# Moving the routing's rank steps, pairing the gathers, and giving the last scatter four banks, in a two-layer decoder trunk with expert routing

## The chip, the cores and the metric

The kernel runs on one core of a Trainium2 chip. The time is the device time of one execution in microseconds (us). The engines are PE (TensorE: matmuls and transposes), DVE (VectorE), ACT (ScalarE), POOL (GpSimd) and SP (SyncE, whose queue issues all weight transfers). PE loads its stationary operand in an instruction of its own (PEld). Results of PE land in PSUM, which has eight banks of 128 x 512 fp32 numbers; DVE and ACT read them from there.

## The reference, cut to what matters

One sequence of 256 tokens with 1024 channels goes through an RWKV-7 time mix, a dense SwiGLU, an RG-LRU block and an expert layer, and a last norm. The change is in the expert layer:

```python
def moe_swiglu(h, w_router, b_router, w_gu, w_d):
    t = h.reshape(B * T, D)
    logits = (t @ w_router + b_router).astype(jnp.float32)
    top_v, top_i = lax.top_k(logits, TOP_K)                      # 2 of 8
    probs = jax.nn.softmax(top_v, axis=-1)
    comb = jnp.einsum('nk,nke->ne', probs, jax.nn.one_hot(top_i, N_EXPERTS))
    out = jnp.zeros_like(t)
    for e in range(N_EXPERTS):
        out = out + comb[:, e, None] * swiglu(t, w_gu[e], w_d[e])  # (silu(g) * u) @ w_d
```

Its output, times a gate, is added to the residual x, and x is normed. All numbers are fp32.

## The kernel before, in words

**Experts and steps.** The router ranks the eight logits of each token; the two best are the token's experts. An expert gets a table of up to 128 tokens. The first expert is fixed (FIRST, expert 7 of the reference). The other seven are ranked by their token counts, and `TURN` gives the order of turns: turns 0, 2, 4, 6 are "big" (tables of 128 tokens), turns 1, 3, 5, 7 (`SMALL`) are "small" (64 tokens). Each turn's hidden width of 3584 is cut into seven pieces of 512, so there are 56 steps (e, j); `steps` lists three big ones and then a small and a big one in turn. A small and a big step are called a pair below. Step (e, j) needs 6 MB of weights, in the order in which `st.add` lists them: the gate and up half, then the down half of the step before.

**One step.** A big step multiplies with weights that are split in two: ACT casts a piece (`wh`), DVE subtracts it from the original (`wl`), and three products with the split tokens (`xh`, `xl`) give 24 matmuls into bank `mg` and 24 into `mu` (`gu_half`, line 2037). A small step multiplies with the raw weights `rw`, 64 columns at a time, gate and up side by side in one bank `mg` (`gu_small`, line 2047): eight groups k of two products, which the trace records as four. Then follow SiLU, the product with the up half (`sl`), four transposes into `hp` (`tpose`, line 2070), their copy to SBUF as `hTh` (ACT) and `hTl` (DVE) in `tparts`, and the second projection `dn` (`down`, line 2138). Step s does its own first projection and, at its end, `down(s - 1)`.

**The order.** Work beside the projections is hung into a plan: `put(s, n, f)` (line 2091) runs f in step s behind its group n (`tick`). Groups 0 to 7 are those of the first projection, 8 to 11 those of `down`. Each engine runs its instructions in the order in which the program issues them, and a weight cast is issued when the stream (`Stream`, line 104) reaches the piece, up to four pieces ahead. `InOrder` forbids the scheduler to reorder while its flag is on, which it is from the routing seam on.

**The routing seam.** The first expert's gather (`first_gather`, line 1816) fills two banks `gp`; ACT and DVE copy them out in turns as `rr` and split them. On DVE the counts `cnt` are copied first, then `softmax` (line 1776) prepares the weights of the two chosen experts. `t_rank` (line 1967, five small instructions on a 7 x 7 table) ranks the experts and `t_sel` (line 1976, ten) turns the ranks into the order of turns, `turn_i`, which SP loads into registers to address the weights from step 3 on. `t_rank` is put at (0, 1) and `t_sel` at (0, 3), inside the first expert step.

**Gathers.** In steps (1, 4), (3, 4) and (5, 4) the next two experts' tokens are gathered. `gather(e, k, w)` (line 2016) is eight products with a one-hot matrix `Pm` into one PSUM bank; `gathered` (line 2028) copies it out on ACT and DVE: two halves for the big expert (`cst` or `other`), two for the small one (`condr`), and the split. There are four such groups, k = 0, 2, 4, 6, at groups 0, 1, 2, 3 of the step, their copies one group later. Their tiles, those of `hp`, of `ptp` (`scatter_cols`, line 1943) and of the scatters carry the tag "m", which alternates between two banks (line 1938). In small steps `tpose` and `tparts` stand at group 4.

**The last scatter.** The last expert's output is multiplied back to token order in four products, two column halves by two token halves (`scatter`, line 2119), and added to x in `onto`. At the end of the program `onto_last` (line 2267) runs product and addition together, one after the other.

Of the kernel before, what the change touches and what calls it, by code (L numbers as in the profile page):

```python
# [7 lines left out]
F32 = mybir.dt.float32  # L8
# [3 lines left out]
AF = mybir.ActivationFunctionType  # L12
ALU = mybir.AluOpType
AX = mybir.AxisListType
PSUM = bass.MemoryType.PSUM

P = 128
# [7 lines left out]
E = 8  # L25
CAP = 128
# [4 lines left out]
HALF = 64  # L31

LEAD = 3

TURN = (3, 0, 4, 1, 5, 2, 6)
# [321 lines left out]
def kernel_body(tc, io, out, dbg=None):  # L357
# [18 lines left out]
    with ctx:  # L376
# [1202 lines left out]
        for c2 in range(4):  # L1579
            ps = lin("x", c2)  # L1580
# [195 lines left out]
        def softmax():  # L1776

            V.tensor_scalar(o1, rank, 0.0, None, ALU.is_equal)
            V.tensor_scalar(o2, rank, 1.0, None, ALU.is_equal)
            V.tensor_reduce(m1, lg, AX.X, ALU.max)  # L1780
            V.tensor_tensor(cmb, o2, lg, ALU.mult)
            V.tensor_reduce(m2, cmb, AX.X, ALU.add)
            V.tensor_tensor(m2, m1, m2, ALU.subtract)
# [53 lines left out]
        def root(i):  # L1837
            S.activation(rs[i], rs[i], AF.Sqrt, bias=eps_n, scale=1.0 / D)

        st.held = []  # L1840
        lo_mm(1, 1, 0, last[0])
        res(0)
# [43 lines left out]
        first_gather(1, range(4), range(1, 2))  # L1886
        first_gather(1, range(4, 8))
        V.tensor_copy(cnt, pps[1][:, E:2 * E])
        softmax()
        lx.close()  # L1890
        dump("x3", xt)
        dump("lg", lg)
# [33 lines left out]
        for k2 in range(5):  # L1926
# [5 lines left out]
            if k2 == 3:  # L1932
                more(1)
                later()

        S.activation(m2, m2, AF.Tanh, scale=0.5)
        st.held = None
        pdn = Turn(pa.pool, bank, m=[4, 5], dn0=[7], dn1=[0], dns=[6])
        pgu = Turn(pa.pool, bank, g=[1], u=[3], gs=[2])
# [17 lines left out]
            onehot(Pms[e], i, e)  # L1957

        Pm2 = {}


        N7 = E - 1
        o7 = oscr.rearrange("p a b c -> p (a b c)")[:, 0:N7 * N7].rearrange("p (b c) -> p b c", b=N7)

        RK = V

        def t_rank():

            a_, b_ = cnt[:, None, 0:N7].broadcast_to([P, N7, N7]), cnt[:, 0:N7, None].broadcast_to([P, N7, N7])
            RK.tensor_tensor(o7, a_, b_, ALU.is_equal)  # L1970
            RK.tensor_tensor(o7, o7, lt8[:, 0:N7, 0:N7], ALU.mult)
            RK.tensor_tensor(sel, a_, b_, ALU.is_gt)
            RK.tensor_tensor(o7, o7, sel, ALU.add)
            RK.tensor_reduce(crank, o7, AX.X, ALU.add)

        def t_sel():
            for k, r in enumerate(TURN):
                RK.tensor_scalar(sel[:, k, :], crank, float(r), None, ALU.is_equal)
            RK.tensor_tensor(o7, sel, iota[:, None, 0:N7].broadcast_to([P, N7, N7]), ALU.mult)
            RK.tensor_reduce(turnf, o7, AX.X, ALU.add)  # L1980
            RK.tensor_copy(turn_i, turnf)

        def t_sort(dst, src):
            V.tensor_copy(dst[:, :, 0:1], src[:, :, FIRST:E])
# [31 lines left out]
        def gather(e, k0, w):  # L2016

            gp[e, k0] = ps = pdn.tile([P, 2, w], F32, tag="m", name=f"gp{e}{k0}", bufs=2)
            for kk in range(2):
                for z, src in enumerate((hh, hl)):  # L2020
                    for i in range(2):
                        mm(ps[:, kk, :], src[:, i, (k0 + kk) * P:(k0 + kk + 1) * P], Pm2[e][:, i, 0:w], z == 0 and i == 0, z == 1 and i == 1)
# [68 lines left out]
        def put(s, n, *fs):  # L2091
            plan.setdefault((s, n), []).extend(fs)
# [5 lines left out]
        def expert_out(e):  # L2098


            yg, parts, ps = {}, {}, {}
            small = e in SMALL
            rows_ = [slice(n * HALF, (n + 1) * HALF) if small else slice(0, P) for n in range(2)]

            def weigh(n):
                yg[n] = other if small or n == 0 else spare
                r = rows_[n]
                V.tensor_tensor(yg[n][r], dps[e][0 if small else n][r], gt2[r, n * 512:(n + 1) * 512], ALU.mult)

            def split(n):  # L2110
                yh = mb.tile([P, 512], F32R, tag="yh", name=f"yh{e}{n}", bufs=1)
                yl = mb.tile([P, 512], F32R, tag="yl", name=f"yl{e}{n}", bufs=1)
                S.copy(yh, yg[n])
                V.tensor_tensor(yl, yg[n], yh.bitcast(F32), ALU.subtract)
                parts[n] = yh, yl
                if small:
                    parts[1] = parts[n]

            def scatter(n, i):
                r = rows_[n]  # L2120
                ps[n, i] = pdn.tile([P, 512], F32, tag="m", name=f"sc{e}{n}{i}", bufs=2)
                l = PTs[e][r, i, :]
                if e == E - 1:
                    mm(ps[n, i], l.bitcast(F32), yg[n][r], True, True)
                else:
                    mm(ps[n, i], l, parts[n][0][r], True, False)
                    mm(ps[n, i], l, parts[n][1][r], False, True)

            def onto(n, i):
                sl = slice(n * 512, (n + 1) * 512)  # L2130
                V.scalar_tensor_tensor(xt[:, i, sl], ps[n, i], cmbq[:, i, e:e + 1], xt[:, i, sl], ALU.mult, ALU.add)

            return [[lambda n=n, f=f: f(n) for n in range(2)] for f in (weigh, split)] + [
                {(n, i): (lambda n=n, i=i, f=f: f(n, i)) for n in range(2) for i in range(2)} for f in (scatter, onto)]
# [36 lines left out]
                S.copy(gt2[:, n * 512:(n + 1) * 512], gt2ps[n])  # L2171

        at = {x: k for k, x in enumerate(steps)}
        put(0, 1, t_rank)
        put(0, 3, t_sel)
        put(0, 6, lambda: t_sort(posq, posm))
        put(1, 0, lambda: t_sort(mskq, msk))

# [13 lines left out]
        for e in SMALL:  # L2192

            if e > 1:
                w, p, sc, add = outs[e - 2]
                t = at[e, 0]
                put(t, 0, *w)
                put(t, 1, p[0])
                for i in range(2):
                    put(t, 6 + 3 * i, *(f[n, i] for f in (sc, add) for n in range(2)))  # L2200
            put(at[e, 1], 2, lambda e=e: scatter_cols(e, V.tensor_copy))
            if e > 1:
                put(at[e, 3], 2, lambda e=e: scatter_cols(e - 1, V.tensor_copy))

            w, p, sc, add = outs[e - 1]
            t = at[e, 8 - LEAD]
            put(t, 0, w[0])
            put(t, 1, p[0], w[1])
            put(t, 6, p[1])
            for n, k in zip((3, 5, 8, 10), sc):  # L2210
                put(t, n, sc[k], add[k])

            if e < E - 1:
                for i in range(2):
                    put(at[e, 3], 5 + i, lambda e=e, i=i: choice(e + 1, i))
                    put(at[e, 3], 8 + i, lambda e=e, i=i: choice(e + 2, i))
                for k in range(0, KT, 2):
                    put(at[e, 7 - LEAD], k // 2, lambda e=e, k=k: gather(e + 1, k, CAP + HALF))
                    put(at[e, 7 - LEAD], k // 2 + 1, lambda e=e, k=k: gathered(e + 1, k))
        w7, _, sc7, add7 = outs[E - 1]  # L2220

        gus = {}
        for s, (e, j) in enumerate(steps):
            now[0] = s
            small = e in SMALL
            gus[s] = [pgu.tile([P, 512], F32, tag="gs" if small else "g", name=f"mg{s}")]
            if s > 0:
                put(s, 4 if small else 1, lambda s=s: tpose(s - 1))
                put(s, 4 if small else 2, lambda s=s: tparts(s - 1))
            if small:  # L2230
                gu_small(e, gus[s][0])
                silu(s)
                times(s)
            else:
                put(s, 5, lambda s=s: silu(s))
                if s > 0:
                    put(s, 9, lambda s=s: times(s))
                gu_half(e, gus[s][0], 0)
            if s == 0:
                scatter_cols(0, S.copy)  # L2240
                weights()
                rx.close()
                mp = ctx.enter_context(tc.tile_pool(name="moe", bufs=1, side="right"))
                mb = ml.enter_context(tc.tile_pool(name="moe3", bufs=1, side="right"))
                gt2 = mp.tile([P, D], F32, name="mgt2")
                st.behind = None
            if not small:
                gus[s].append(pgu.tile([P, 512], F32, tag="u", name=f"mu{s}"))
                gu_half(e, gus[s][1], 4)
            if s == 0:  # L2250
                st.load()
                turns()
            if s == len(steps) - 1:
                down(s - 1, range(2))
                tpose(s)
                tparts(s)
                down(s - 1, range(2, 4))
                down(s)
                preload(AF.Sqrt)
                for f in w7:  # L2260
                    f()
            elif s > 0:
                down(s - 1)
            else:
                times(0)
        assert not plan, plan.keys()
        onto_last = {k: lambda k=k: (sc7[k](), add7[k]()) for k in sc7}

        o = rawC.tile([P, 2 * D], F32, tag="raw", name="fo").rearrange("p (i d) -> p i d", i=2)

# [155 lines left out]
```

## Time and profile before

| | us |
|---|---|
| time, median of 3 runs (1482.25 to 1483.77) | 1483.29 |
| the profiled execution: its own time | 1483.4 |
| its span, first to last instruction | 1481.6 |
| PE busy | 1418.6 (96%) |
| DVE busy | 1015.3 (69%) |
| ACT busy | 755.4 (51%) |
| weights moved | 488.53 MB |

The experts take from about 619 us to 1467 us. Nearly all instructions are recorded by one helper, so their line is L99 and they are told apart by their tiles. Matmuls are pipelined, and a PE that is "busy" is not at its peak, so the start times in the chain of waits say more than the busy sums. Of two engines with little idle time the chain tells which one the other waits for.

### The profile page before, as it was taken

What the parts mean: (1) busy time and instruction counts of PE and PEld (TensorE: products, weight loads), DVE (VectorE), ACT (ScalarE), POOL (GpSimd) and SP (SyncE); (2) the same over time, 40 slices, a digit from 0 to 9 for tenths busy, and PEclk for the clock granted to TensorE, in tenths of its full rate; (3) what the DMA queues carried; (4) which work ended last, traced back from release to release, by engine and by line L of the source; (5) the groups of instructions that cost most, each with busy time, mean ns of one, the idle gap of its engine ahead of it and who ended that gap; (6) DMA issues with size and microseconds to landing.
All of it is one profiled execution on the core that took longest, in us unless ns stands there. A gap on an engine that the chain in (4) does not pass through costs nothing.

```text
span 1481.6 us, 20752 instructions
## 1 busy us (share of the span) xinstructions
PE 1418.6 (96%) x7751; PEld 994.3 (67%) x7751; DVE 1015.3 (69%) x1534; ACT 755.4 (51%) x1124; POOL 52.5 (4%) x44
## 2 busy tenths in 40 slices
PE   4998989899999899999999999999999999999996
PEld 2784685899999798776566655665566555665652
DVE  7788978777879689685565666655665556666543
ACT  3666524544444567575455544545455455554432
POOL 3002520000000000000000000000000000000000
PEclk9999979899999899899999999999999999999998
DMA  9564235988889355488999999999999999999993
GB/s 372 181 240 170 87 115 227 349 341 309 312 295 394 136 173 190 177 330 337 412 422 421 393 405 421 421 421 419 408 419 421 421 421 418 406 422 422 421 417 124
DMA packets 69934, 488.53 MB, mean 330 GB/s; under 512 B 8000, under 2 KB 8384, under 8 KB 11968
## 3 DMA queue, kind: packets, MB, share of 16 engines
q1 hardware_dynamic: 69824, 487.11, 82.6%
q8 instruction: 63, 1.03, 0.3%
q14 instruction: 47, 0.39, 0.1%
HBM read 486.03 MB, written 1.05 MB: 329 GB/s over the span
## 4 chain that ended last, share of the span: by engine, by line
PE 86%; DVE 7%; ACT 3%; DMA 2%; issue 1%; SPq 0%; POOL 0%; DVEq 0%; ACTq 0%
PE mg L99 23%; PE dn L99 18%; PE fgu L99 11%; PE mu L99 10%; PE fd L99 5%; PE psr L99 2%; PE linx L99 2%; PE hp L99 2%; PE v L99 2%; DMA rq<-ada 2%; DVE rq L99 1%; PE u L99 1%; DVE wl L99 1%; PE psk L99 1%; PE po L99 1%
## 5 line engine op out<-in xcount | busy, mean ns | idle before, releaser
L99 DVE TENSOR_TENSOR wl<-rw,wh 128x1024 fp32r<-128x1024 f32 x444 | 533.7, 1221 | 126.5 <-ACT wh L99 122.0
L99 ACT CAST wh<-rw 128x1024 fp32r<-128x1024 f32 x444 | 461.1, 1050 | 237.6 <-PE dn L99 56.5
L99 PE MATMUL mg<-rw,condr 128*64 128x512 f32 x896 | 210.4, 599 | 0.0
L99 PEld LDWEIGHTS mg<-rw,condr 128*64 128x64 f32 x896 | 58.8, 136 | 105.7 <-issue 98.3
L99 PE MATMUL fgu<-fxh,wh 128*128 128x256 f32 x448 | 127.8, 286 | 1.2 <-ACT fxh L99 1.2
L99 PE MATMUL fgu<-fxl,wh 128*128 128x256 f32 x448 | 127.7, 285 | 0.0
L99 PE MATMUL fgu<-fxh,wl 128*128 128x256 f32 x448 | 127.2, 284 | 0.0
L99 PE MATMUL dn<-rw,hTh 128*64 128x512 f32 x448 | 102.9, 599 | 0.5 <-ACT hTh L99 0.5
L99 DVE TENSOR_TENSOR sl<-sl,mu 128x512 f32<-128x512 f32 x28 | 19.2, 687 | 116.0 <-PE mu L99 106.7
L99 PE MATMUL dn<-wh,hTh 128*128 128x512 f32 x224 | 91.6, 409 | 2.4 <-ACT hTh L99 2.4
L99 PE MATMUL mg<-wh,xh 128*128 128x512 f32 x224 | 91.7, 409 | 0.1
L99 PE MATMUL dn<-wh,hTl 128*128 128x512 f32 x224 | 88.8, 396 | 0.0
L99 PE MATMUL mg<-wl,xh 128*128 128x512 f32 x224 | 88.6, 396 | 0.0
L99 PE MATMUL dn<-wl,hTh 128*128 128x512 f32 x224 | 88.3, 394 | 0.0
L99 PE MATMUL mg<-wh,xl 128*128 128x512 f32 x224 | 88.1, 393 | 0.0
L99 PE MATMUL mu<-wh,xh 128*128 128x512 f32 x224 | 88.0, 393 | 0.0
L99 PE MATMUL mu<-wl,xh 128*128 128x512 f32 x224 | 87.6, 391 | 0.0
L99 PE MATMUL mu<-wh,xl 128*128 128x512 f32 x224 | 87.4, 390 | 0.0
L99 PEld LDWEIGHTS fgu<-fxh,wh 128*128 128x128 f32 x448 | 85.5, 191 | 2.0 <-ACT fxh L99 1.6
L99 PEld LDWEIGHTS fgu<-fxl,wh 128*128 128x128 f32 x448 | 85.5, 191 | 0.7 <-issue 0.5
L99 PEld LDWEIGHTS fgu<-fxh,wl 128*128 128x128 f32 x448 | 85.8, 191 | 0.2 <-issue 0.2
L99 ACT CAST hTh<-hp 128x512 fp32r<-128x512 f32 x28 | 16.4, 586 | 133.8 <-PE hp L99 133.8
(419 smaller groups left out, 2386.6 us busy)
## 6 DMA issues: line engine op xcount, KB each, us to landing
rw<-moe_gu SPq DMA_DIRECT2D x224, 1024.0 KB, 11.2
rw<-moe_d SPq DMA_DIRECT2D x106, 1024.0 KB, 11.1
rw<-ffn_gu SPq DMA_DIRECT2D x28, 1024.0 KB, 7.6
rw<-ada SPq DMA_DIRECT2D x28, 1024.0 KB, 8.2
rq<-ada SPq DMA_DIRECT2D x19, 1024.0 KB, 4.9
rw<-ffn_d SPq DMA_DIRECT2D x14, 1024.0 KB, 6.1
rw<-lru_in SPq DMA_DIRECT2D x8, 1024.0 KB, 7.9
rw<-moe_d SPq DMA_DIRECT2D x12, 512.0 KB, 13.5
```

Of the source, the lines that this page charges most:

```text
L99: r = f(*a, **k)
```

## The change

Three things, with no change in what is computed:

- `t_rank` and `t_sel` move ahead of the first expert step, to the place of `softmax`, behind the copy of `cnt`. `softmax` and the tanh that follows it move into the step, to (0, 1).
- The gathers k = 0, 2 stand together at group 0 and k = 4, 6 at group 4, their copies at groups 1 and 5. In small steps `tpose` and `tparts` move from group 4 to group 2.
- The last expert's four scatter products get a bank each (those of tags g, u, dn0, dn1) and are issued one after the other; the four additions keep their places.

```diff
@@ -1886,7 +1906,8 @@
         V.tensor_copy(cnt, pps[1][:, E:2 * E])
-        softmax()
+        t_rank()
+        t_sel()
         lx.close()
@@ -1932,8 +1953,6 @@
-        S.activation(m2, m2, AF.Tanh, scale=0.5)
...
@@ -2118,7 +2115,10 @@
             def scatter(n, i):
                 r = rows_[n]
-                ps[n, i] = pdn.tile([P, 512], F32, tag="m", name=f"sc{e}{n}{i}", bufs=2)
+                if e == E - 1:
+                    ps[n, i] = (pdn if i else pgu).tile([P, 512], F32, tag=("gu", ("dn0", "dn1"))[i][n], name=f"sc{e}{n}{i}")
+                else:
+                    ps[n, i] = pdn.tile([P, 512], F32, tag="m", name=f"sc{e}{n}{i}", bufs=2)
@@ -2171,8 +2171,8 @@
-        put(0, 1, t_rank)
-        put(0, 3, t_sel)
+
+        put(0, 1, softmax, lambda: S.activation(m2, m2, AF.Tanh, scale=0.5))
...
@@ -2215,8 +2215,9 @@
                 for k in range(0, KT, 2):
-                    put(at[e, 7 - LEAD], k // 2, lambda e=e, k=k: gather(e + 1, k, CAP + HALF))
-                    put(at[e, 7 - LEAD], k // 2 + 1, lambda e=e, k=k: gathered(e + 1, k))
+                    n = (0, 0, 4, 4)[k // 2]
+                    put(at[e, 7 - LEAD], n, lambda e=e, k=k: gather(e + 1, k, CAP + HALF))
+                    put(at[e, 7 - LEAD], n + 1, lambda e=e, k=k: gathered(e + 1, k))
@@ -2225,8 +2226,9 @@
             if s > 0:
-                put(s, 4 if small else 1, lambda s=s: tpose(s - 1))
-                put(s, 4 if small else 2, lambda s=s: tparts(s - 1))
+                n = 2 if small else 1
+                put(s, n, lambda s=s: tpose(s - 1))
+                put(s, 2, lambda s=s: tparts(s - 1))
@@ -2264,7 +2266,9 @@
-        onto_last = {k: lambda k=k: (sc7[k](), add7[k]()) for k in sc7}
+        for k in ((0, 0), (1, 0), (0, 1), (1, 1)):
+            sc7[k]()
+        onto_last = add7
```

At the routing seam this is DVE's row of work, from the copy of the counts (`wrs` holds `cnt`, `crank` and `turnf`; `cst` is the table; `rr` is the first expert's gather on its way out of `gp`). Before:

```order
L99 COPY wrs<-pps_5860 128x8
L99 TENSOR_SCALAR o_5755<-rank 128x16
L99 TENSOR_SCALAR o_5756<-rank 128x16
L99 TENSOR_REDUCE m_5753<-lg 128x2
L99 TENSOR_TENSOR cmb<-o_5756,lg 128x16
L99 TENSOR_REDUCE m_5754<-cmb 128x2
L99 TENSOR_TENSOR m_5754<-m_5753,m_5754 128x2
L99 TENSOR_SCALAR rr<-gp_5750,mods 128x128 x2
```

After:

```order
L99 COPY wrs<-pps_5860 128x8
L99 TENSOR_TENSOR cst_2286<-wrs 128x49
L99 TENSOR_TENSOR cst_2286<-cst_2286 128x49
L99 TENSOR_TENSOR cst_2286<-wrs 128x49
L99 TENSOR_TENSOR cst_2286<-cst_2286 128x49
L99 TENSOR_REDUCE wrs<-cst_2286 128x7
L99 TENSOR_SCALAR cst_2286<-wrs 128x7 x7
L99 TENSOR_TENSOR cst_2286<-cst_2286,cst 128x49
L99 TENSOR_REDUCE wrs<-cst_2286 128x7
L99 CAST turn_i<-wrs 128x7
L99 TENSOR_SCALAR rr<-gp_5750,mods 128x128 x2
```

Fifteen small instructions stand ahead of the first copy of `gp` where six stood. The six softmax instructions now follow the third weight subtraction of the first expert step, and on ACT the tanh (`m`) moves with them. ACT at the same place, before:

```order
L99 CAST wh_5933<-rw_5931 128x1024
L99 CAST xh_5937<-rr 128x256
L99 ACTIVATE m_5754<-m_5754 128x2
L99 CAST wh_5943<-rw_5931 128x1024
L99 CAST wh_5955<-rw_5953 128x1024
L99 CAST wh_5970<-rw_5953 128x1024
```

After:

```order
L99 CAST wh_5942<-rw_5940 128x1024
L99 CAST xh_5946<-rr 128x256
L99 CAST wh_5951<-rw_5940 128x1024
L99 CAST wh_5963<-rw_5961 128x1024
L99 ACTIVATE m_5754<-m_5754 128x2
L99 CAST wh_5980<-rw_5961 128x1024
```

The tanh stands two weight casts later. In the first step with gathers this is PE's row of work from the last two gather groups to the transposes, before:

```order
L99 MATMUL mg_7270<-rw_7227,condr 64x512
L99 MATMUL mg_7270<-rw_7237,condr 64x512
L99 MATMUL gp_7321<-Pm_7114,mhh 128x192 x2
L99 MATMUL gp_7321<-Pm_7114,mhl 128x192 x2
L99 MATMUL gp_7321<-Pm_7114,mhh 128x192 x2
L99 MATMUL gp_7321<-Pm_7114,mhl 128x192 x2
L99 MATMUL mg_7270<-rw_7227,condr 64x512
L99 MATMUL mg_7270<-rw_7237,condr 64x512
L99 MATMUL gp_7340<-Pm_7114,mhh 128x192 x2
```

And after, from the second gather group of the first two:

```order
L99 MATMUL gp_7292<-Pm_7114,mhh 128x192 x2
L99 MATMUL gp_7292<-Pm_7114,mhl 128x192 x2
L99 MATMUL gp_7292<-Pm_7114,mhh 128x192 x2
L99 MATMUL gp_7292<-Pm_7114,mhl 128x192 x2
L99 MATMUL mg_7270<-rw_7227,condr 64x512
L99 MATMUL mg_7270<-rw_7237,condr 64x512
L99 MATMUL mg_7270<-rw_7227,condr 64x512
L99 MATMUL mg_7270<-rw_7237,condr 64x512
L99 MATMUL hp_7321<-vec,sl_7235 128x128 x4
L99 MATMUL mg_7270<-rw_7227,condr 64x512
L99 MATMUL mg_7270<-rw_7237,condr 64x512
```

Gather groups no longer alternate with groups of `mg`, and the transposes stand between the two pairs. In a small step ACT's row changes like this (a piece of the difference; `rw_6472` and the tile behind it are the down weights):

```order
-L99 CAST wh_6487<-rw_6472 128x1024
-L99 CAST wh_6493<-rw_6491 128x1024
-L99 CAST hTh_6504<-hp_6499 128x512
+L99 CAST hTh_6490<-hp_6485 128x512
+L99 CAST wh_6496<-rw_6472 128x1024
+L99 CAST wh_6502<-rw_6500 128x1024
 L99 ACTIVATE sl_6516<-mg_6467 64x512
```

The copy of the transposes moves ahead of two weight casts; DVE's `hTl` moves in the same way ahead of their two subtractions.

## Rows read from the trace of the kernel before

**Rows 1.** Waits of PE, 619 to 1482 us: total us, times, longest us

```profile
PE dn L99 <- ACT hTh L99: 2.9, 4, 0.8
PE hp L99 <- DVE sl L99: 2.0, 1, 2.0
```

**Rows 2.** Engines by stretch (us, busy, PEclk, DMA share, GB/s); DMA from 712 to 1448

```profile
872.00:1060.00 188.00, 187.20 (x847) 113.92 (x846) 116.02 (x122) 97.99 (x121) 0.00 (x0) 1.00 1.01 421
...
988.83:1199.97 211.14, 210.34 (x949) 126.89 (x950) 129.10 (x135) 108.04 (x131) 0.00 (x0) 1.00 1.01 418
...
DMA packets 42757, 306.90 MB, mean 417 GB/s; under 512 B 4742, under 2 KB 4742, under 8 KB 5903
```

**Rows 3.** Chain of waits (start us, us, what) through the first gather step

```profile
790.00 0.86 PE mg L99 x4
790.86 1.07 PE gp L99 x8
791.93 1.01 PE mg L99 x4
...
803.27 6.11 PE dn L99 x24
```

**Rows 4.** Chain of waits through a plain small step

```profile
855.72 4.29 PE mg L99 x20
860.01 0.59 PE hp L99 x4
...
863.32 5.75 PE dn L99 x24
```

**Rows 5.** Chain of waits through a small step with ptp

```profile
914.50 2.58 PE mg L99 x12
917.07 0.37 PE ptp L99 x2
917.44 1.87 PE mg L99 x8
```

**Rows 6.** Timeline of ACT and PE in the first gather step

```profile
792.90 0.70 ACT L99 ACTIVATE condr<-gp,mods 128x64 f32<-128x64 f32 x2 [0.48 <-DVE cst L99]
...
797.94 2.00 ACT L99 CAST wh<-rw 128x1024 fp32r<-128x1024 f32 x2
...
803.27 0.50 PE L99 MATMUL dn<-wh,hTh 128*128 128x512 f32 x1 [0.80 <-ACT hTh L99]
```

**Rows 7.** Timeline of DVE at the seam and in the first expert step

```profile
615.98 0.24 DVE L99 TENSOR_SCALAR o<-rank 128x16 f32<-128x16 f32 x2
...
616.66 0.16 DVE L99 TENSOR_TENSOR m<-m,m 128x2 f32<-128x2 f32 x1
...
618.06 0.41 DVE L99 TENSOR_SCALAR rr<-gp,mods 128x128 f32<-128x128 f32 x1 [1.24 <-ACT rr L99]
...
626.30 0.20 DVE L99 TENSOR_TENSOR cst<-wrs 128x49 f32<-128x49 f32 x1
...
627.40 2.35 DVE L99 TENSOR_TENSOR wl<-rw,wh 128x1024 fp32r<-128x1024 f32 x2
...
629.67 0.59 DVE L99 TENSOR_SCALAR cst<-wrs 128x7 f32<-128x7 f32 x7
...
630.86 0.36 DVE L99 TENSOR_SCALAR m<-m 128x2 f32<-128x2 f32 x2
```

**Rows 8.** Timeline of ACT and PE in the first two expert steps

```profile
625.47 1.06 ACT L99 CAST wh<-rw 128x1024 fp32r<-128x1024 f32 x1 [0.34 <-PE mg L99]
...
637.37 0.66 PE L99 MATMUL hp<-vec,sl 128*128 128x128 f32 x4 [1.98 <-DVE sl L99]
```

**Rows 9.** Timeline of PE and DVE at the last scatter

```profile
1467.55 3.88 PE L99 MATMUL sc<-other,PT 64*128 64x512 f32 x8 [0.79 <-DVE other L99]
...
1471.04 0.16 DVE L99 TENSOR_TENSOR ssq<-ssq 128x1 f32<-128x1 f32 x1 [0.79 <-ACT fo L99]
1471.11 1.40 DVE L99 SCALAR_TENSOR_TENSOR xt<-sc,wr,xt 128x512 f32<-128x512 f32 x2
```

More of the change, by code (lines that the diff above doesn't have):

```diff
@@ L1838, in root, with t_rank, t_sel @@
             S.activation(rs[i], rs[i], AF.Sqrt, bias=eps_n, scale=1.0 / D)
+        N7 = E - 1
+        o7 = oscr.rearrange("p a b c -> p (a b c)")[:, 0:N7 * N7].rearrange("p (b c) -> p b c", b=N7)
+        def t_rank():
+            a_, b_ = cnt[:, None, 0:N7].broadcast_to([P, N7, N7]), cnt[:, 0:N7, None].broadcast_to([P, N7, N7])
+            V.tensor_tensor(o7, a_, b_, ALU.is_equal)
+            V.tensor_tensor(o7, o7, lt8[:, 0:N7, 0:N7], ALU.mult)
+            V.tensor_tensor(sel, a_, b_, ALU.is_gt)
+            V.tensor_tensor(o7, o7, sel, ALU.add)
+            V.tensor_reduce(crank, o7, AX.X, ALU.add)
+        def t_sel():
+            for k, r in enumerate(TURN):
+                V.tensor_scalar(sel[:, k, :], crank, float(r), None, ALU.is_equal)
+            V.tensor_tensor(o7, sel, iota[:, None, 0:N7].broadcast_to([P, N7, N7]), ALU.mult)
+            V.tensor_reduce(turnf, o7, AX.X, ALU.add)
+            V.tensor_copy(turn_i, turnf)
         st.held = []
@@ L1959, in kernel_body @@
         Pm2 = {}
[L1962 to L1981, printed above, removed]
         def t_sort(dst, src):
```

## The prediction

> **What bounds the kernel now.** I read first who waits for whom, from the routing seam (the end of the gathers for the first expert, 619 us) to the end. PE has three entries there, the largest a product of the second projection (dn) that waits for the transposed hidden activations hTh, 2.9 us in 4 cases; none names a DMA [rows 1]. Then the chain of waits: through the expert steps it is one product on PE after the other [rows 3 to 5]. So PE is short of time there, not of data, and an edit counts where it shortens PE's row of work or what PE waits for. It is a near thing: in an undisturbed stretch the 16 DMA engines show a share of 1.01 and move 421 GB/s, one period of seven pairs of steps with a gather in it takes 211.14 us at 418 GB/s, and from 712 to 1448 us the mean is 417 GB/s [rows 2]. The transfers have 736 x (1 - 417/421) = 7.0 us of idle in that stage and no more.
>
> **Gathers two at a time (three steps).** The chain through a step with a gather: at 790.00 four records of the small expert's mg (0.86), then a block of eight gather products (1.07), four of mg (1.01), and so on; the next dn begins at 803.27 and takes 6.11 [rows 3]. A plain small step has twenty mg from 855.72 (4.29), four transposes hp (0.59), twelve mg, and a dn of 5.75 from 863.32 [rows 4]: 7.60 + 5.75 = 13.35. The gather step takes 13.27 + 6.11 = 19.38, so a gather costs 6.03 us.
> I split the 6.03. Four records of mg take 0.86 in a run and 1.01 behind an interruption [rows 3]: 0.15 for coming back. Going over costs as much: two transposes take 0.37 [rows 5] and four take 0.59 [rows 4], so 0.11 each and 0.15 fixed. One interruption is thus 0.30. The four blocks cost 4 x (1.07 + 0.15) = 4.88; the other 1.15 is a stall. The timeline shows it: ACT runs two weight casts (2.00 us from 797.94) ahead of the last group's evacuation, hTh stands behind that, and dn waits 0.80 us for it [rows 6]; the rest is inside the longer dn.
> After the change two interruptions of sixteen records are left, each (1.07 - 0.15) x 2 + 0.30 = 2.14, together 4.28: **0.60 saved**. The stall: hp now comes after three groups of mg instead of five, and the order on ACT puts hTh ahead of the two casts and of the last two groups. PSUM alternates between two banks: gather 0, gather 2, hp, gather 4, gather 6. Today the first group's bank is read out 1.67 us after its block ends (791.93 to 793.60, the end of ACT's copies) [rows 3, 6]. hp needs that bank, while PE has a second block and eight mg to do, 2.8 us. Gather 6 needs hp's bank, free some 1.8 us after hp (two reads of its 512 columns and the end of the second group's evacuation), while PE has eight mg and gather 4 in front of it, 2.8 us. The last two groups are evacuated beside dn and first read a whole dn later (5.75). So I take the whole **1.15** as gone; were it kept, the sum falls by 3.4. Per gather 1.75, three gathers: **-5.2 us**.
>
> **hp two groups earlier (28 small steps).** By itself this moves four transposes within a row of equal work: 0 on PE. But in seven steps the transposes of a one-hot matrix (ptp) already stand at that place, and today they interrupt by themselves: 2.58, 0.37, then 1.87 where eight uninterrupted mg would be 1.72 [rows 5]. Side by side with hp they share one interruption: 7 x 0.30 = **-2.1 us** (0 if the switch is paid for each kind of transpose). What the move adds: in the 26 small steps that follow a big one two weight casts (2.00 us) [rows 6] now stand behind hTh on ACT, for the third and fourth piece of dn. From hp's end PE has five groups of mg, 4.3 us, and two pieces of dn, 2.9, before it wants the third. hTh (some 0.6 by its half size), one cast (1.0) and one subtraction (1.2) [rows 6, 7] take 2.8 of these 7.2. Covered by 4.4 us, so 0; the third rival has it uncovered.
>
> **Ranks ahead of the first expert step.** On DVE the ranks take 1.10 us (626.30 to 627.40) and the turns 1.19 (629.67 to 630.86), 2.29 in all; the softmax that they replace at the seam takes 0.84 (615.98 to 616.82) [rows 7]. At the seam they begin at some 616.1, behind the copy of the counts on which they depend, and end at about 618.4, so the evacuation that DVE begins at 618.06, as soon as ACT lets it, begins at about 618.49 [rows 7]: PE's first expert product comes **0.43 us later**.
> In exchange DVE has 2.29 - 0.84 = 1.45 us less to do before 637.37, where PE waits 1.98 us for DVE [rows 8]. I do not count that. The tanh, today in ACT's row ahead of the casts, now stands among them and waits for the softmax, which DVE reaches only behind a weight subtraction that ends at 626.30. So the cast that ACT begins at 625.47 today [rows 8] begins at about 627.3, 1.85 us later; DVE waits some 1.3 for it, and the 1.45 is down to 0.15 or less. I take +0.43. The ends: -1.0 (DVE's saving arrives whole) and +2.3 (ACT's 1.85 arrives whole). SP reads the turns some 12 us earlier and can issue the weights behind them earlier; one transfer now stands behind that read. PE waits for no transfer there, so 0.
>
> **Last scatter.** Four banks instead of two. Today the four products end at 1467.55 + 3.88 = 1471.43. But DVE's second pair of additions stands behind the sum of squares at 1471.04, which waits for ACT, not PE, and the last of them begins after 1471.7 [rows 9]: 0.
> Here the Trainium skill says otherwise. "Perfetto Trace Analysis", section Optimizing Tensor Performance, Matmuls, wants independent groups of matmuls to rotate through different PSUM banks so that one group's evacuation overlaps the next group's products; by that rule the tail should shorten, by my estimate at most 0.4 us, to 1476.1. In this trace the additions wait for ACT, and the sum stands without it.
>
> **Sum.** -5.2 - 2.1 + 0.4 = -6.9. The profiled execution took 1483.4 us (span 1481.6), 0.1 above the median of 1483.29, so the forecast is **1476.5 us**.
>
> **The rivals.** *The transfers take over.* The period of 211.14 us becomes 211.14 - 1.75 - 0.60 = 208.8 on PE (one gather, two merged ptp), while its bytes at 421 GB/s take 211.14 x 418/421 = 209.6 [rows 2]. If the ring's lead is used up, 0.8 us of each of 736/211 = 3.5 periods is lost: 1479.4. For it: the share of 1.01. Against it: no wait of PE for a DMA today [rows 1].
> *Merging saves nothing*, because the switch is paid per group whatever stands beside it. Then 3 x 1.15 - 0.43 = 3.0 us stay: 1480.4.
> *The transfers bind outright.* Then PE time is free time, and only the seam's 0.43 counts: 1483.8. The DMA share speaks for it [rows 2], the waits of PE against [rows 1]. The Trainium skill's "Perfetto Trace Analysis", section Identifying the Most-Contended Engine, would have the most contended resource worked on first and does not trust matmul busy time; "DMA: Bandwidth & Descriptors", section Where 436 GB/s comes from, gives a ceiling of 435 GB/s, close above the measured 421. By that rule the DMA is the bound and this forecast fails.
> *Slower: late casts.* If the two casts behind hTh reach dn too late, the stall of today's gather steps appears in the other 23 as well: 23 x 1.15 = 26.5, against 3 x 0.60 + 2.1 = 3.9 saved, plus 0.4: 1483.4 + 23.0 = 1506.4. It decides once ACT or DVE have over 4.4 us of other work between hp and dn. The steps with scatters come closest, and they stall nowhere today [rows 1].
> *The seam doesn't hide ACT's delay:* +2.3 in place of +0.4, 1478.4; that is in the range.
>
> **How the numbers follow.** Forecast (1475 to 1478.5) 0.60; transfers take over in part, 1479.4, 0.15; merging saves nothing, 1480.4, 0.10; transfers bind, 1483.8, 0.08; late casts 0.04; a better seam, near 1475, 0.03. A measurement of this kernel can tell about 0.2%, 3.0 us, from no change, so faster means under 1480.3. Faster: 0.60 + 0.15 + 0.03 and 0.04 of the case at the border, 0.82. Same: 0.06 + 0.08 = 0.14. Slower 0.04. The range runs from DVE's whole saving at the seam with all else as forecast (1476.5 - 1.4 = 1475.1, and 0.5 for the spread of the runs) to the case without merging: 1474.6 to 1480.6.
>
> **What would show it.** Right: the gather step shows two blocks of sixteen records of about 2.0 us and a dn of about 5.75 without a wait for hTh; the seven ptp stand beside hp with twenty mg behind them; the PE wait for hTh falls from 2.9 us to about 0.5; a period of seven pairs takes about 208.8 us at 421 GB/s; PE's wait of 1.98 for DVE stays within 0.5. Wrong: waits of PE or of the casts for rw tiles that grow from 900 us on (transfers), a dn that waits for wh or wl in small steps (late casts), or a gather pair that costs what two single blocks did (merging).

## The result and the profile after

The changed kernel takes **1475.7 us** (median of 6 runs, 1474.64 to 1476.58), the kernel before, in runs beside it, 1483.12 (1482.25 to 1484.74): a ratio of 0.9949, 95% interval 0.9936 to 0.9962. The forecast was 1476.5. The profiled execution took 1475.25, 8.15 less than the one of before, and its span falls from 1481.6 to 1473.4.

Three marks in both traces divide these 8.2 us: DVE's copy of the counts at the seam (615.90 before, 615.03 after), the first hp (637.37 and 636.46), and the start of the last sixteen records of dn (1463.11 and 1454.95). Up to the copy both kernels are the same, so its 0.87 us is scatter between executions. From the copy to hp it is 21.47 and 21.43, from hp to the last dn 825.74 and 818.49, from there to the end of the span 18.49 and 18.45. **The change's gain is 7.25 us, and all of it lies between the first hp and the last dn.**

The waits of PE after, 600 to 1475 us (waiter, what it waits for: total us, times, longest), against [rows 1]:

```profile
PE hp L99 <- DVE sl L99: 1.8, 1, 1.8
...
PE dn L99 <- ACT hTh L99: 0.5, 1, 0.5
```

The wait for hTh went from 2.9 us in 4 cases to 0.5 in one, the last step's. The chain of waits through the first gather step after (start us, us, what), against [rows 3]:

```profile
788.78 0.86 PE mg L99 x4
789.64 1.96 PE gp L99 x16
791.60 1.87 PE mg L99 x8
793.47 0.59 PE hp L99 x4
794.06 1.87 PE mg L99 x8
795.92 1.96 PE gp L99 x16
797.89 2.73 PE mg L99 x12
800.61 5.79 PE dn L99 x24
```

The two blocks of sixteen take 1.96 each where four of eight took 1.07 each. From the first mg to the end of dn it is 17.62 us, 1.76 less than the 19.38 before. The timeline of ACT in this step shows why dn no longer waits (start us, us, engine, operation, out<-in; in brackets what it waited for):

```profile
794.41 0.59 ACT L99 CAST hTh<-hp 128x512 fp32r<-128x512 f32 x1
794.89 2.01 ACT L99 CAST wh<-rw 128x1024 fp32r<-128x1024 f32 x2
797.04 0.46 ACT L99 ACTIVATE cst<-gp,mods 128x128 f32<-128x128 f32 x1
```

hTh is done 5.6 us ahead of dn; the casts and the evacuation of the last groups, which stood ahead of it in [rows 6], come behind. A step with ptp, against [rows 5]:

```profile
1120.34 2.58 PE mg L99 x12
1122.91 0.37 PE ptp L99 x2
1123.28 0.44 PE hp L99 x4
1123.72 4.44 PE mg L99 x20
```

Before, the rows that follow those of [rows 5] are:

```profile
919.31 0.59 PE hp L99 x4
919.89 2.73 PE mg L99 x12
```

The four rows after take 7.82 us, to the start of dn; the five before took 8.12. Engines by stretch (us, busy and count of PE, PEld, DVE, ACT, POOL; PEclk, DMA share, GB/s), one period of seven pairs:

```profile
985.26:1194.10 208.84, 208.84 (x949) 127.19 (x950) 129.49 (x135) 107.70 (x131) 0.00 (x0) 1.00 1.01 421
```

The period fell from 211.14 to 208.84 us, and the transfers now run at 421 GB/s through it. PE waits for none of them, but ACT does: the waits of its weight casts for moe_d between 900 and 1460 us, before and after, are:

```profile
ACT wh L99 <- DMA rw<-moe_d: 7.4, 10, 1.7
...
ACT wh L99 <- DMA rw<-moe_d: 51.1, 33, 6.3
```

### The profile page after: what moved, and what is told of

Same layout as the page of the kernel before. It is cut to its first block, busy times and chain, and to the rows that moved or that the text cites. A ratio compares the mean times of both kernels' runs of the same rounds, so it can differ in the third digit from the quotient of the medians.

```text
span 1473.4 us, 20722 instructions
## 1 busy us (share of the span) xinstructions
PE 1409.8 (96%) x7751; PEld 992.7 (67%) x7751; DVE 1017.5 (69%) x1534; ACT 753.5 (51%) x1124; POOL 52.6 (4%) x44
## 4 chain that ended last, share of the span: by engine, by line
PE 85%; DVE 9%; ACT 3%; DMA 1%; issue 1%; SPq 0%; POOL 0%; DVEq 0%; ACTq 0%
PE mg L99 24%; PE dn L99 18%; PE fgu L99 11%; PE mu L99 10%; PE fd L99 5%; PE psr L99 2%; PE hp L99 2%; PE linx L99 2%; DVE rq L99 2%; DVE s L99 2%; PE u L99 1%; PE psk L99 1%; DMA rq<-ada 1%; PE po L99 1%; DVE wl L99 1%
```

## The experiments

All start from the changed kernel. "Distance" is from the start of the first hp to the start of the last run of dn, in the profiled execution; it leaves out the scatter ahead of the seam. Seven kernels that are alike over this way (the change, e9, e4, e5, e8, e10, e11) have a distance of 818.49 to 818.51 us, so it repeats to some 0.02 us. The times alone, with intervals of about 2 us each way, could not tell e1 or e3 from the change.

| kernel | time, us | first hp | last dn | distance | against the change | expected | casts' wait for moe_d, 900 to 1460 |
|---|---|---|---|---|---|---|---|
| before | 1483.1 | 637.37 | 1463.11 | 825.74 | +7.25 | +7.3 | 7.4 |
| the change | 1475.7 | 636.46 | 1454.95 | 818.49 | | | 51.1 |
| e1: unpaired | 1477.2 | 635.84 | 1456.29 | 820.45 | +1.96 | +1.8 | 18.6 |
| e2: old gather steps | 1480.6 | 637.15 | 1460.96 | 823.81 | +5.32 | +5.2 | 12.6 |
| e3: hp late | 1477.4 | 636.23 | 1456.67 | 820.44 | +1.95 | +2.1 | 15.9 |
| e6: hp in two | 1483.1 | 637.22 | 1462.81 | 825.59 | +7.10 | +8.4 | 3.5 |
| e12: cut in eight steps | 1468.4 | 637.46 | 1449.09 | 811.63 | -6.86 | -6.9 | 58.6 |
| e7: cut in all 28 | 1465.7 | 636.08 | 1444.15 | 808.07 | -10.42 | -6 to -10 | 133.5 |

**e1: only the merging undone.** Ratio to before 0.996 (0.9946 to 0.9974).

```
-                    n = (0, 0, 4, 4)[k // 2]
+                    n = (0, 1, 4, 5)[k // 2]
```

> The changed kernel with the four gather blocks of a gather step apart again, after mg groups 0, 1, 4 and 5, and hp where the change has it, after group 2: only the merging is undone. By my theory (an interruption of the mg row costs 0.30 us, the stall came from hTh's place on ACT) each of the three gather steps grows by 2 x 0.30 = 0.60, from 17.62 to 18.22 us, hTh still ahead of the last dn without a wait: +1.8 us, 1477.5. Rival, the stall of 1.15 belongs to single blocks, not to hp's place: 3 x 1.75 = +5.2 us, 1480.9, with dn waiting for hTh. Rival, merging saves nothing: 0, 1475.7.

The chain through its gather step from the first block on:

```profile
789.05 1.07 PE gp L99 x8
790.11 1.01 PE mg L99 x4
791.12 1.07 PE gp L99 x8
792.19 1.01 PE mg L99 x4
793.20 0.59 PE hp L99 x4
```

From the first mg (788.19) to the end of dn the step takes 18.24 us (18.22 expected), and dn waits for hTh in no step but the last. So the merging saves 0.6 us a gather, and the stall does not come from single blocks.

**e2: the gather steps as they were.** Ratio 0.9982 (0.9972 to 0.9991).

```
-                    n = (0, 0, 4, 4)[k // 2]
+                    n = k // 2
...
-                n = 2 if small else 1
+                n = (4 if j == 7 - LEAD and e < E - 1 else 2) if small else 1
+                p = n if small else 2
...
-                put(s, 2, lambda s=s: tparts(s - 1))
+                put(s, p, lambda s=s: tparts(s - 1))
```

> The changed kernel with its three gather steps as they were: four blocks after groups 0 to 3, hp after group 4 there, everything else of the change kept. By my theory the whole gather term comes back, 3 x 1.75 = +5.2 us, 1480.9, each gather step 19.38 us again, and dn waits some 0.8 us for hTh in each. Rival, part of that gain was hp's move in the other steps or lies in transfers: less than +3 us. With the transfers in part the bound, the PE row grows and the casts' waits for transfers, 51 us from 900 to 1460 in the changed kernel, shrink to some 10 us or less.

The whole term is back, 5.32 us, and with it the wait that the change removed:

```profile
PE dn L99 <- ACT hTh L99: 2.9, 4, 0.8
```

e1 and e2 together split the term: 1.96 for the merging and 5.32 - 1.96 = 3.36, 1.12 a gather, for what stands ahead of hTh, against 3 x 0.60 and 3 x 1.15 in the forecast. e2 moves hp and the last two gather blocks together, so which of the two makes the stall is not separated.

**e3: hp after the fifth group in the other steps.** Ratio 0.9964 (0.9951 to 0.9976).

```
-                n = 2 if small else 1
+                n = (2 if j == 7 - LEAD and e < E - 1 else 4) if small else 1
+                p = n if small else 2
...
-                put(s, 2, lambda s=s: tparts(s - 1))
+                put(s, p, lambda s=s: tparts(s - 1))
```

> The changed kernel with hp after group 4 again in all small steps but the three with a gather: ptp and hp interrupt apart. By my theory 7 x 0.30 = +2.1 us, 1477.8: the row of a ptp step goes from 7.82 back to 8.12 us. Rival, the switch is paid for each kind of transpose: 0, 1475.7. Rival, the early hp is a cost by the casts behind hTh: below 1475.7.

```profile
911.60 2.58 PE mg L99 x12
914.17 0.37 PE ptp L99 x2
914.54 1.87 PE mg L99 x8
916.41 0.59 PE hp L99 x4
```

Above is its chain through a step with ptp: two interruptions again. 1.95 us over seven steps is 0.28 a step. The early hp has no cost of its own: dn waits for wh or wl in neither kernel.

**e6: one more interruption in each small step.** Ratio 1.000 (0.999 to 1.001).

```
...
-                put(s, n, lambda s=s: tpose(s - 1))
-                put(s, 2, lambda s=s: tparts(s - 1))
+                if small:
+                    put(s, 2, lambda s=s: tpose(s - 1, range(2)))
+                    put(s, 3, lambda s=s: tpose(s - 1, range(2, 4)), lambda s=s: tparts(s - 1))
...
```

> The changed kernel with the four transposes of hp in two pairs, after groups 2 and 3, in all 28 small steps: the same products and one more interruption in each. By my theory (0.15 us to go over to transposes and 0.15 to come back, whatever stands in the interruption) 28 x 0.30 = +8.4 us, 1484.1, with a pair of transposes at 0.37 us and a group of mg behind each at 1.01. Rival, an interruption costs nothing and only the count of products matters: 0, 1475.7. Rival, PE has slack behind the transfers: less than +4 us.

Chain through a plain step (857 us), and through a step in which a scatter product stands after the same group (826 us):

```profile
827.78 0.67 PE sc L99 x2
828.45 0.22 PE hp L99 x2
...
857.56 0.37 PE hp L99 x2
857.93 1.01 PE mg L99 x4
858.94 0.37 PE hp L99 x2
```

The plain step shows what was expected, 0.37 for each pair and 1.01 for the group behind. The sum, 7.10, is below 8.4 because four of the 28 second pairs fell beside a scatter. Three of them take 0.22 there and share its interruption both ways; the fourth, transposes of a small expert's step, takes 0.27 there as it does elsewhere, and shares at most the way back. 24 x 0.30 = 7.2 is the estimate for the others. The same products, only divided differently, take back the whole gain of the change.

**e5: the last scatter in two banks again.** Time 1475.84, ratio 0.9946 (0.993 to 0.9961).

```
-                    ps[n, i] = (pdn if i else pgu).tile([P, 512], F32, tag=("gu", ("dn0", "dn1"))[i][n], ...)
+                    ps[n, i] = pdn.tile([P, 512], F32, tag="m", name=f"sc{e}{n}{i}", bufs=2)
...
-        for k in ((0, 0), (1, 0), (0, 1), (1, 1)):
-            sc7[k]()
-        onto_last = add7
+        onto_last = {k: lambda k=k: (sc7[k](), add7[k]()) for k in sc7}
```

> The changed kernel with the last scatter's four products in two banks by turns again. By my theory (the last additions wait for ACT's sum of squares, not for PE) 0: 1475.7, and from the start of the last dn to the end of the span 18.4 to 18.5 us. Rival, by the rule of rotating banks: +0.4 us, 1476.1.

1475.84 against 1475.70 is no difference that the runs can tell, but the rival's 0.4 lies within their spread too; the traces of the kernels before and after decide. In the changed kernel the timeline of PE and DVE at this place, against [rows 9], is:

```profile
1459.39 2.71 PE L99 MATMUL sc<-other,PT 64*128 64x512 f32 x8 [0.79 <-DVE other L99]
...
1462.81 0.16 DVE L99 TENSOR_TENSOR ssq<-ssq 128x1 f32<-128x1 f32 x1 [0.79 <-ACT fo L99]
1462.89 1.40 DVE L99 SCALAR_TENSOR_TENSOR xt<-sc,wr,xt 128x512 f32<-128x512 f32 x2
```

PE finishes the four products in 2.71 us in place of 3.88, and DVE's second pair of additions stands where it stood, 7.94 us behind the start of the last dn (8.00 before), behind the sum of squares that waits 0.79 us for ACT. The profiled execution of e5 can't be laid beside it: its granted clock over these products is 0.73, where every other one shows 1.00, and its products take 4.83 us.

**e4, e9, e10 and e11: four forms of the seam.** e4 puts softmax and tanh back at the seam and ranks and turns into the step; e9 is the changed kernel again; e10 (and e8, the same kernel on another chip) moves the tanh:

```
-        put(0, 1, softmax, lambda: S.activation(m2, m2, AF.Tanh, scale=0.5))
+        put(0, 1, softmax)
+        put(0, 3, lambda: S.activation(m2, m2, AF.Tanh, scale=0.5))
```

e11 has softmax and ranks at the seam, and tanh and turns after the fourth group:

```
+        softmax()
         t_rank()
-        t_sel()
...
-        put(0, 1, softmax, lambda: S.activation(m2, m2, AF.Tanh, scale=0.5))
+        put(0, 3, lambda: S.activation(m2, m2, AF.Tanh, scale=0.5), t_sel)
```

> The changed kernel with the softmax and the tanh at the seam again and ranks and turns in the first expert step: only that part is undone. By the forecast (+0.43 us for the new place) it is 0.4 us faster, 1475.3. Rival, DVE's saving of 1.45 us arrives whole at hp: 1.0 us slower, 1476.7. Rival, ACT's delay arrives whole: 2.3 us faster, 1473.4. The trace of the changed kernel suggests some 0.1 us slower, since the first hp begins 0.14 us earlier than in the kernel before, counted from a place ahead of the seam. The trace decides by the start of the first hp counted from the last gather of the seam.

> The changed kernel with the tanh alone two groups of products later in the first expert step, so that ACT's casts don't wait for the softmax on DVE. By my theory the wait of 2.06 us on ACT and the 1.21 us of DVE behind it go, and the first hp begins up to 1.2 us earlier, of its wait of 1.8: 1474.5 at best, at least 1475.2. Rival, hp waits for something else (the gate of PE's clock, transfers): 1475.7 with hp where it was.

> The changed kernel itself, once more, beside the two other versions of the seam on one chip: 1475.7 us as before, some 21.43 us from DVE's copy of the counts at the seam to the first hp.

> The changed kernel with the tanh two groups of products later, once more. If its gain is the missing wait of ACT (0.9 to 1.2 us ahead of the first hp at like clock), it is 0.9 to 1.2 us faster than the changed kernel on the same chip. If the gain of its first run lay ahead of the edit (its profiled execution reached the seam 1.7 us earlier and took no less from there on), the two agree within 0.5 us.

> The changed kernel with softmax and ranks at the seam and only the turns and the tanh in the first expert step, after its fourth group. DVE's work at the seam takes 0.84 + 1.10 = 1.94 us in place of 2.29, so the first expert product comes some 0.1 us after the old place instead of 0.4, and the wait of ACT for DVE's softmax is gone; DVE does 1.19 us in the step instead of 0.84. By my theory the first hp comes as early as with the tanh later or up to 0.3 us earlier: 1474.4 to 1474.8. Rival, the turns in the step cost what the softmax cost: 1475.7.

| kernel | time (lowest to highest) | ratio to before, interval | copy to first product | copy to hp | PE's wait for DVE at hp |
|---|---|---|---|---|---|
| before | 1483.1 | | 3.41 | 21.47 | 1.98 |
| the change | 1475.70 (1474.64 to 1476.58) | 0.9949 (0.9936 to 0.9962) | 3.92 | 21.43 | 1.84 |
| e9 | 1475.33 (1474.73 to 1475.99) | 0.9948 (0.9934 to 0.9961) | 3.93 | 21.43 | 1.83 |
| e4 | 1475.23 (1475.06 to 1476.53) | 0.9944 (0.993 to 0.9957) | 3.42 | 21.39 | 1.94 |
| e8 | 1473.71 (1473.41 to 1474.88) | 0.9932 (0.9918 to 0.9945) | 3.92 | 21.59 | 0.63 |
| e10 | 1474.16 (1473.22 to 1474.59) | 0.9937 (0.9924 to 0.9951) | 3.92 | 21.53 | 0.63 |
| e11 | 1474.85 (1472.97 to 1475.10) | 0.9939 (0.9925 to 0.9953) | 3.42 | 20.81 | 1.47 |

The timeline of the changed kernel from the seam to the first hp:

```profile
615.03 0.16 DVE L99 COPY wrs<-pps 128x8 f32<-128x8 f32 x1
...
617.63 0.17 DVE L99 CAST turn_i<-wrs 128x7 int32<-128x7 f32 x1
617.71 0.40 DVE L99 TENSOR_SCALAR rr<-gp,mods 128x128 f32<-128x128 f32 x1
...
618.95 0.80 PE L99 MATMUL mg<-wh,xh 128*128 128x512 f32 x1 [0.58 <-ACT xh L99]
...
626.50 0.20 ACT L99 ACTIVATE m<-m 128x2 f32<-128x2 f32 x1 [2.06 <-DVE m L99]
...
627.67 2.36 DVE L99 TENSOR_TENSOR wl<-rw,wh 128x1024 fp32r<-128x1024 f32 x2 [1.21 <-ACT wh L99]
...
636.46 0.66 PE L99 MATMUL hp<-vec,sl 128*128 128x128 f32 x4 [1.84 <-DVE sl L99]
```

Each link is as described: DVE's turns end at 617.8, the evacuation follows at once, the first product comes 0.51 us later than before (0.43 forecast); the tanh waits 2.06 us for DVE, and DVE 1.21 us for the cast behind it. But hp comes no later. DVE's last three subtractions ahead of it begin 15.66 us behind the copy before and 15.62 after:

```profile
631.56 3.49 DVE L99 TENSOR_TENSOR wl<-rw,wh 128x1024 fp32r<-128x1024 f32 x3
...
630.65 3.49 DVE L99 TENSOR_TENSOR wl<-rw,wh 128x1024 fp32r<-128x1024 f32 x3
```

e4 and the change agree in copy to hp, and in time within the spread of their runs, so **this part of the change is worth nothing that shows, in either direction**.

With the tanh later, the wait on ACT is gone, PE's wait at hp falls by 1.2 us, and the time by 1.2 us on the same chip as e9; the slowest run of e10 is under the fastest of e9, and the slowest of e8 under the fastest of e4 beside it. Copy to hp doesn't show it, as the clock differs. Engines by stretch in e9, e10 and e3, over six us from the first product:

```profile
618.85:624.85 6.00, 6.00 (x20) 4.85 (x21) 5.08 (x10) 4.70 (x8) 0.00 (x0) 0.76 0.00 0
...
617.86:623.86 6.00, 6.00 (x14) 4.76 (x15) 4.59 (x9) 4.13 (x8) 0.00 (x0) 0.52 0.00 0
...
617.64:623.64 6.00, 6.00 (x14) 4.72 (x15) 4.58 (x9) 4.12 (x8) 0.00 (x0) 0.51 0.00 0
```

The fair comparison is e3, whose seam is that of the change and whose granted clock over these six us is 0.51: it takes 22.51 us from the copy to hp (e2, at 0.51 too, 22.52), so e10 is 0.98 us ahead of it. Between the profiled executions of e9 and e10 themselves, the whole 0.98 us lies ahead of the copy (614.92 and 613.94), so the tanh's gain rests on the times and on this comparison at like clock; no single pair of traces shows it. All five runs of e10 lie below the six of the changed kernel, though the intervals of the two ratios overlap. e11 also begins its first product as early as before, and reaches hp 0.62 us sooner; its time is 0.5 us lower, with runs that overlap those of e9.

**e12 and e7: less work on PE.** Both leave out one of the eight groups of mg products, e12 in 8 of the small steps, e7 in all 28; the weights are still transferred.

```
-                    for z in range(2):
+                    for z in range(0 if k == 6 and steps[now[0]][1] in (1, 5) else 2):
```

(e12; in e7 the condition is k == 6 alone)

> The changed kernel that leaves out one of the eight groups of mg products (the seventh 128 rows of the contraction) in 8 of the 28 small steps, with all weights still transferred: 8 x 0.86 = 6.9 us less on PE. If the transfers' lead still covers it (leaving it out in all 28 won 10 us): 6 to 7 us faster, 1469 to 1470, and the casts' waits for transfers from 900 to 1460 us lie between the 51 us of the changed kernel and the 133 of that cut. If the transfers already bind in part: under 3.5 us, 1472 or more.

> The changed kernel that leaves out one of the eight groups of mg products (the seventh 128 rows of the first projection's contraction) in all 28 small steps, with all weights still transferred: 28 x 0.86 = 24.1 us less on PE. If PE alone were the bound: 1451.6. If transfers take over as soon as their lead is used up: they run without idle to about 1447 us in the changed kernel, and some 11 us lie between their end and the end of the last dn, so no more than about 6 to 10 us is won, 1466 to 1470, and PE shows waits for rw from some point after 900 us on. If the lead was used up already (transfers take over in part): under 3 us, 1473 or more.

e12 is 6.9 us faster than e9 on the same chip (ratio to before 0.9899, 0.9884 to 0.9914): another 6.9 us on PE still arrive whole, and PE waits for no transfer. e7 takes 24.1 us (28 x 0.86) off PE and wins 10.0 (0.9879, 0.9864 to 0.9894). How the transfers stop it is seen at one of its gather steps:

```profile
1198.37 1.99 ACT L99 CAST wh<-rw 128x1024 fp32r<-128x1024 f32 x2 [12.00 <-DMA rw<-moe_d]
...
1203.54 0.70 ACT L99 ACTIVATE condr<-gp,mods 128x64 f32<-128x64 f32 x2 [1.26 <-DVE cst L99]
...
1204.30 1.12 PE L99 MATMUL hp<-vec,sl 128*128 128x128 f32 x4 [4.78 <-ACT condr L99]
```

A cast waits 12.0 us for its weights, the gather's evacuation stands behind it on ACT, and hp needs the bank that this evacuation frees. PE loses 4.78 us there to a transfer that its own list of waits doesn't name. In all that list has 9.4 us in e7 that it doesn't have in the changed kernel: 6.4 for condr, 2.1 for hTl and 0.9 for hTh. The end of the transfers is seen in the DMA row from 1430 to 1465 us, in 40 slices of 0.875 us (the mean busy share of the DMA engines in tenths), of the kernel before, the change, e12 and e7:

```profile
DMA  9999999999999999999999999741000000000000
```

```profile
DMA  9999999999999999987642100000000000000000
```

```profile
DMA  9999999999999999767642000000010001427970
```

```profile
DMA  9999999999999876643100001000072992000000
```

It falls under half at about 1452.8, 1447.5, 1447.5 and 1444.9 us; the last dn ends at 1466.8, 1458.6, 1452.8 and 1448.05. So the transfers' lead at the end was 14.0 us, is 11.1 now, and is 5.3 in e12 and 3.2 in e7 (the last rise in these two is the output).

The casts' waits measure this lead badly. e4, e5, e8, e10 and e11 share the change's distance and have a lead of 10.5 to 11.9 us, and their casts wait 16 to 29 us for moe_d where those of the change and of e9 wait 51 and 53. What makes that difference is open; it costs PE nothing in any of them.

## Why the forecast came out, step by step

**What bounds the kernel: right.** PE's row set the time, as [rows 1] had it: e6 gives the gain back with divided transposes alone, and e12 wins 6.9 us with less PE work. The Trainium skill's rule ("Perfetto Trace Analysis", section Identifying the Most-Contended Engine) would have put the DMA first, at 417 to 421 GB/s. Its share is 1.01 in every one of these kernels, and 14 us of PE time still came through (7.25 and 6.86), so the trace disagrees for this kernel up to there. It agrees for e7, where 14 of 24 us are lost.

**Gathers two at a time: right, -5.28 (3 x 1.76) for -5.2.** Merging is 0.65 a gather by e1 (0.60 in the forecast), the stall 1.12 by e2 less e1 (1.15). That hTh's place behind the casts and the last evacuations made the stall was read from one timeline; e1, which keeps the single blocks, has hTh ahead of both and shows no stall, bears it out.

**hp two groups earlier: right, -1.95 by e3 for -2.1.** The price of an interruption holds: 0.28 by e3, 0.296 by e6 (7.10 / 24), and it is paid once for ptp and hp together, or, in three cases of four, for a scatter and hp. The rival that pays for each kind falls with e3. The cover of the casts behind hTh held.

**The seam: the links right, the path wrong, 0 for +0.43.** The delay of the first product was put on the path at its full size. But behind it PE waits 1.98 us for DVE at hp [rows 8], so a product that starts later only uses up a part of that wait. What counts there is DVE's row. Counted from the copy, it starts its evacuations 0.52 us later and its third subtraction only 0.18 later, as fewer of PE's products run at half speed (granted clock over six us from the first product 0.69 before, 0.75 after); then it loses 1.21 us to the cast behind the tanh and has 1.45 us less to do; together hp moves by -0.04. The forecast saw both DVE terms and cancelled them, and then counted PE's 0.43 beside them. Summed at hp by its own terms, 0.43 + 1.3 - 1.45, it would have been some 0.3; what PE's clock gives back was not among them.

**Last scatter: right, 0.** From the last dn to the start of the last scaling of the output it is 11.64 us after and 11.71 before. The Trainium skill's rule on rotating banks ("Perfetto Trace Analysis", section Optimizing Tensor Performance, Matmuls) holds for PE, which is 1.17 us sooner done, and not for the time: the trace's additions wait for ACT.

**The transfers: not reached, but for another reason than given.** One of the forecast's signs of being wrong did come, casts' waits for transfers that grow (7.4 to 51.1 us), and no time was lost to it. The forecast weighed 209.6 us of bytes against 208.8 us on PE and held the rival off because PE waited for no DMA. The period is 208.84, at 421 GB/s with nothing idle, and the casts' waits grow (longest 3.7 us between 900 and 1000, 6.3 from 1400 on): the transfers do fall behind. The working named the ring's lead and did not measure it. The transfers ended 14.0 us ahead of PE and now end 11.1 ahead; the 2.9 between agree with a loss of 0.8 us a period over 3.5 periods, paid out of the lead. e12 draws it down to 5.3 without harm; e7 shows its end.

**Range.** Faster than 1480.3 and inside 1474.6 to 1480.6. Of the 0.8 us between forecast and median 0.43 is the seam's and 0.28 the starting point (1483.4, where the median of six runs beside the change is 1483.12); the rest is scatter. That it came so close is in part luck: the part ahead of the seam moved by 0.87 us in the profiled executions, with no edit there.

## What to carry to other kernels

Small products that interrupt a long row of another shape are cheapest in company: here one interruption cost 0.28 to 0.33 us (e3, e6, e1), whether gathers, transposes of a one-hot matrix or transposes of activations stood in it, so count interruptions, and put small work beside other small work. A delay is summed at the next place where the path's engine waits for another one, not where it arises. When an engine's share is full but nobody on the path waits for it, measure its lead (when its work ends against when the last of it is used) before believing that it binds, and look for its first damage in the queue that waits for it, not on PE.

## What the runs showed of the hardware

The granted clock at the seam comes back at different times for the same code. In e9 it is 0.76 over the six us from the first product, in e3, with the same seam, 0.51, which is the lower of the two levels (1.2 GHz) nearly throughout; a product of 128x512 takes 0.63 us there and 0.39 after. That moves the first hp by 1.1 us (21.43 and 22.51 us from the copy). The executions with the late return (e2, e3, e8, e10) took 24.6 to 24.8 us from the first to the last start of `linx<-lxh,wh`, products of the RG-LRU block that begin some 100 us ahead of the seam, the others 25.1 to 25.3. From the first of these products to the copy they took 100.4 to 100.6 us, the others 100.8 to 101.1, so they came to the seam sooner and gave it back there. What sets the moment stays open. In e7 the clock falls after PE stood still: over the five us from 1204.30, behind the wait of 4.78, it is 0.57.

```profile
1204.30:1209.30 5.00, 5.00 (x16) 1.98 (x17) 3.35 (x6) 3.97 (x8) 0.00 (x0) 0.57 1.01 419
```
